# A hybrid decoder step on one core: gated products in halves, a sum split from its matmul, and one tile turned a step later

## The chip, the cores and the metric

The kernel runs on one core of a Trainium2 chip. The metric is device time in microseconds (us) of one execution. The core's engines are named as in the profile: PE is TensorE's matmuls and PEld its weight loads, DVE is VectorE, ACT is ScalarE, POOL is GpSimd, and SP is SyncE, whose queue issues nearly all transfers.

## The reference

The kernel computes one layer of a decoder trunk for 1024 prompt rows and 8 sample rows (one new row for each of 8 sequences), all in float32, with a model width of 1024. Cut to what matters:

```python
xn = _rmsnorm(h, pre_g)
proj = jnp.einsum('bld,de->ble', xn, w_in)          # w_in is 1024 x 7168
u, v, z_a, x_b, z_b, g_a, g_b = jnp.split(proj, SPLITS, axis=-1)
u = jax.nn.gelu(u)
vn = _layernorm(jax.nn.gelu(v), ln_g, ln_b)
y_a = u * _chunk_spatial_mix(vn, w_s, b_s) * jax.nn.silu(z_a)
pooled, new_pool = _pool_branch(x_b, prev_pool, pos0, w_pool, pool_scale)
y_b = pooled * jax.nn.silu(z_b)
m = sigmoid(g_a) * (y_a @ w_pa) + sigmoid(g_b) * (y_b @ w_pb)
h = h + _rmsnorm(m @ w_out, post_g)
h = h + _rmsnorm(sigmoid(_rmsnorm(h, ple_in_g) @ w_pg) * (p @ w_ple), ple_out_g)
```

Three places of it concern the change. The first is the gated branch, `y_a`: a product of three factors for every channel and row. The second is the pool branch of the sample rows, whose trailing windows reach back into the last 15 rows of each sequence (`state_pool`); their sums over the window are needed. The third is the second norm of h and the product with `w_pg`, whose operand is h turned to have channels on the partitions.

## The kernel before

**Tiles and products.** Everything is cut into tiles of 128 partitions. Activations stand turned, channels on partitions and rows along the free axis: a block of 128 channels is 128 x 1032, for 1024 prompt rows and 8 sample rows. A pair of two such blocks of the result is computed by Strassen's seven products, whose operands are sums and differences of quarters of the weights and of the activations (names such as T1 to T4, B11, B21, B22 are such quarters or sums: `xT3` is one of the activations, `wgB21` one of `w_pg`). The operands are split in a high and a low part (`h` and `l` in a name), and three matmuls are done for each pair. In a timeline a product is a run of 12 matmuls 512 wide, or of 24 that are 260 wide where the half with the sample rows is concerned. Each product lands in a region of PSUM of two banks, of which three rotate (`acc`, in the last two products `acct`), and is added into its result by DVE or ACT: an instruction such as `u<-acc,u` does that, and the region may be written again afterwards. Two more single banks serve everything else (`pht`, `state`, `mix`).

**What DVE does for the products.** It makes the operands' sums and low parts (`zaw`, `zas`, `uw`, `us`, `hw`, `hs`, 512 wide each), the sums into results, and the elementwise work.

**The gated branch.** Class ZA (from line 1060) is what becomes of the results z_a. `done` (lines 1063 to 1073) multiplies, for each of the two 128-channel blocks of a pair, z by u (128 x 1032), makes the mixed block, multiplies z's 1024 prompt columns with it, and its 8 sample columns with the samples' mix. There are four pairs, so eight blocks. In the timeline these are the rows `za<-za,u` and `za<-za,big`.

**The past rows.** `pool_state` (line 1087) sets a 128 x 1024 space to zero and loads the past rows of the 8 sequences into it by small transfers. `state_sums` (line 1103) adds them up along the free axis (a TENSOR_REDUCE from 128 x 1024 to 128 x 128), and multiplies the result on PE with the constant `twice`, which adds two halves of the partitions and turns the result; then DVE copies it to `past`.

**h, turned.** After the product with `w_out` the tiles of h are finished two at a time: `out_finish` (norm and residual), `gate_norm` (the sum of squares of the next norm), and `gate_input` (line 1441), which turns a tile: for the tiles concerned here eight 128 x 128 transposes on PE into two `pht` banks and two ACT copies to `big`. The last two tiles, 7 and 6, are turned at the first pair's products with `w_pg`.

**What sets the order.** Nothing is issued when it is written. The code calls the operations on a recorder, Planner (lines 56 to 300), which keeps what each reads and writes. `at(step, f)` attaches work f to a step, a step being one of the products in PE's sequence; the planner derives from that a due time for each operation. `order` then goes through time with a table of estimated durations and gives each engine the next operation by these due times; PE's products are fixed in their main sequence, and the rest, the transfers of SP's queue with it, fits in where the estimate says. `play` (line 296) issues it all, so nearly every row of the profile has L299. A small edit may thus reorder a wide stretch on several engines.

Of the kernel before, what the change touches and what calls it, by code (L numbers as in the profile page):

```python
# [13 lines left out]
ALU = mybir.AluOpType  # L14

P = 128
D = 1024
NB = D // P
# [282 lines left out]
@with_exitstack  # L301
def tile_hybrid_step(ctx, tc, *args):
    hybrid_step(ctx, tc, *args)


def hybrid_step(
# [7 lines left out]
    nc = tc.nc  # L314
# [24 lines left out]
    def bank(name):  # L339
        n_name[0] += 1  # L340
        return plan.tile(bankp.tile([P, 512], F32, tag="bank", name=f"{name}_{n_name[0]}"), "bank")
# [22 lines left out]
    def mul(out, a, b):  # L364
        nc.vector.tensor_tensor(out=out, in0=a, in1=b, op=ALU.mult)
# [6 lines left out]
    nc = plan  # L372
# [6 lines left out]
    big = cpool.tile([P, NB, T], F32, tag="big", name="big")  # L379
# [34 lines left out]
    class Operand:  # L414
# [37 lines left out]
        def at(self, what, k):  # L452
            return [part[:, k % 2, :] for part in self.parts[what, k // 2]]
# [144 lines left out]
    def halves(t, j):  # L598

        return Features.like(t[:, HALF:]) if j else t[:, :HALF]  # L600
# [90 lines left out]
    class User:  # L691
# [37 lines left out]
        def done(self):  # L729
            pass  # L730
# [63 lines left out]
    def sample_stationary(src, nk, gain=None):  # L794

        st = slot("sst", (P, nk, P), F32R)
        nc.gpsimd.memset(f32(st), 0.0)
        ps = bank("psst").rearrange("p (k t) -> p k t", t=16)
        for k in range(nk):
            nc.tensor.transpose(ps[:, k, :NS], src[:NS, k * P : (k + 1) * P], ident[:NS, :NS])  # L800
        got = ps[:, :nk, :NS]
        if gain is not None:
            mul(smix_s, got, gain.unsqueeze(2).to_broadcast([P, NB, NS]))
            got = smix_s
        split(got, st[:, :, :NS], st[:, :, 32 : 32 + NS])
        return st
# [54 lines left out]
    NPAIR = NB // 2  # L861
# [198 lines left out]
    class ZA(User):  # L1060
        func = AF.Silu

        def done(self):
            u = us.pop(self.pair)
            for m, z in enumerate(self.out):
                b = 2 * self.pair + m
                mul(z, z, u[m])
                zt, mixed = z[:, :SEQ].rearrange("p (t c) -> p t c", c=P), big[:, :, b * P : (b + 1) * P]
                nc.vector.scalar_tensor_tensor(out=mixed, in0=mixed, scalar=lncol[:, 0, b : b + 1],
                                               in1=lnt["off"][:, b].unsqueeze(1).to_broadcast([P, NB, P]),  # L1070
                                               op0=ALU.mult, op1=ALU.add)
                mul(zt, zt, mixed)
                mul(z[:, SEQ:], z[:, SEQ:], smix_s[:, b, :])

        def store(self):
# [24 lines left out]
    state_sb, tail = big[:, 7, :D], big[:, 6, :D]  # L1100
    past = cpool.tile([P, NB, NS], F32, tag="past", name="past")

    def state_sums():

        got = big[:, 4, :P]
        nc.vector.tensor_reduce(out=got, in_=state_sb.rearrange("p (r c) -> p c r", c=P),
                                op=ALU.add, axis=mybir.AxisListType.X)
        ps = bank("state")
        nc.tensor.matmul(ps[:, : P // 2], got, twice, start=True, stop=True)
        nc.vector.tensor_copy(past, ps[:, : P // 2].rearrange("p (b t) -> p b t", b=NB))  # L1110
# [121 lines left out]
    bsteps, xusers = [], []  # L1232
# [5 lines left out]
    flat, c = big.rearrange("p b t -> p (b t)"), [T + 4 * w for w in (0, HALF, HALF + WIDE, HALF + 2 * WIDE)]  # L1238
# [20 lines left out]
    c = vsteps[0]  # L1259
# [11 lines left out]
    for i, u in enumerate(vusers):  # L1271

        nxt = vsteps[1][1:] + vsteps[2] if i == 0 else (vsteps[i + 1] if i + 1 < NPAIR else gasteps[0])
# [20 lines left out]
    for i, z in enumerate(zausers):  # L1294
        at(uflow[14 * (i + 1) + 1], z.store)
    at(bsteps[0][0][2], pool_state)
    at(bsteps[0][0][4], state_sums)
    for g, u in enumerate(xusers):
        at(bsteps[g][1][4], u.tails)
        for i in range(2):  # L1300
# [26 lines left out]
    p, l, c = gbsteps[2], gbsteps[3], pasteps[0]  # L1327
    turn_over(yaop, l, [*l[1:], c[0]])
    p, l, c = pasteps[2], pasteps[3], pbsteps[0]
# [78 lines left out]
    def out_finish(t):  # L1408
        r = rows(t)
        h = h_of[t][:r]  # L1410
        rs = rstd(parts.pop(t), r)
        nc.vector.scalar_tensor_tensor(out=h, in0=h, scalar=rs[:r], in1=gains["post"][:r],
                                       op0=ALU.mult, op1=ALU.mult)
        nc.gpsimd.dma_start(out=h, in_=x_of(t), accum_op=ALU.add)
        dma(kept["h"][t * P : t * P + r, :], h)
# [5 lines left out]
    def words_of(t):  # L1421
        return big.bitcast(U16)[:, :, 2 * t * P : 2 * (t + 1) * P]

    def gate_norm(t):

        r = rows(t)
        h = h_of[t]
        n, spare = sm("ssq"), slot("hspare", (P, D))[:r] if t == S else big[:, :, t * P : (t + 1) * P]
        src = h[:r] if t == S else h.rearrange("p (k c) -> p k c", c=P)
        nc.scalar.activation(out=spare, in_=src, func=AF.Square, scale=D ** -0.5, accum_out=n[:r])  # L1430
        root(n, r, rin(t))
        if t not in BY_DMA:
            return
        words = slot("hw", (P, 2, D), U16)
        for w in range(2):
            nc.scalar.activation(out=words[:, w], in_=h.bitcast(U16).rearrange("p (c w) -> p w c", w=2)[:, w],
                                 func=AF.Copy)
        h_of[t] = h.bitcast(U16).rearrange("p (k t) -> p k t", t=P)
        nc.sync.dma_start_transpose(out=h_of[t], in_=words.rearrange("p w c -> p (w c)"))

    def gate_input(t):

        got = h_of.pop(t)
        if t == S:
            samples["h"] = sample_stationary(got, NB)
            return
        for k4 in (slice(0, 4), slice(4, NB)):
            if t in BY_DMA:
                nc.scalar.activation(out=words_of(t)[:, k4].rearrange("p k (t w) -> p k t w", w=2),
                                     in_=got.rearrange("p (w k) t -> p k t w", w=2)[:, k4], func=AF.Copy)  # L1450
                continue
            ps = bank("pht")
            for k in range(4):
                nc.tensor.transpose(ps[:, k * P : (k + 1) * P], got[:, (k4.start + k) * P : (k4.start + k + 1) * P], ident)
            nc.scalar.activation(out=big[:, k4, t * P : (t + 1) * P], in_=ps.rearrange("p (k t) -> p k t", t=P),
                                 func=AF.Copy)
# [72 lines left out]
    def embed_gate_sample():  # L1529
        ge_start(S)  # L1530
        for j, o in enumerate(sample_product(samples["h"], wgop)):
# [9 lines left out]
    gatesteps = [strassen(Turned(i, "h"), wgop, Embed(i), Tokens, LAST if i == NPAIR - 1 else None)  # L1541
                 for i in range(NPAIR)]
# [5 lines left out]
    l, c = pbsteps[3], outsteps[0]  # L1548
    turn_over(woop, l, [*l[2:], c[0], c[1]], ("B11", "T3", "T2", "B21", "T4", "T1", "B22"))
    l, c = outsteps[3], gatesteps[0]  # L1550
# [13 lines left out]
    for i in range(NPAIR):  # L1564
        nxt = outsteps[i + 1] if i + 1 < NPAIR else gatesteps[0]
        ts = [2 * i + 1, 2 * i]
        at(nxt[0], lambda ts=ts: [out_finish(t) for t in ts])
        at(nxt[1], lambda ts=ts: [gate_norm(t) for t in ts])
        at(nxt[6], lambda ts=ts: [gate_input(t) for t in ts])


    we = Moving(w_ple, 2, "we")
# [200 lines left out]
```

## Time and profile before

| | |
|---|---|
| median of 3 runs | 991.16 us (990.98 to 991.76) |
| the profiled execution's own time | 991.0 us |
| its span, first to last instruction | 989.3 us |
| granted TensorE clock, mean | 0.998 |
| busy: PE, PEld, DVE, ACT, POOL | 975.0, 875.3, 797.4, 529.6, 69.9 us |
| transfers | 174.53 MB, mean 176 GB/s |

The profile is of one execution. A timeline row gives start, duration, engine, line, operation, what is written and read (buffer numbers left out), the shapes, and how many equal instructions the row holds; in brackets stands idle time of the engine before it and what ended it. Matmuls overlap in the array, so a row's duration is longer than the distance to the next one's start; the starts tell the rate. A view of waits lists, for an engine, which waits were ended by what: total us, how often, the longest.

### The profile page before, as it was taken

The numbers are of one execution on the slowest core, as the hardware profiler recorded it, in microseconds if no ns is written. First come the engines' busy times: TensorE is split into PE (matmuls) and PEld (weight loads), VectorE is DVE, ScalarE is ACT, GpSimd is POOL, SyncE is SP. The second block draws the span as 40 slices with busy tenths as digits, with TensorE's granted clock in tenths as the row PEclk, the third lists the DMA queues.
The fourth block names the chain that finished last, engine by engine and source line by source line (L and its number), as shares of the span: only waits on it lengthen the run. The fifth ranks groups of instructions, "written<-read, shape, count | busy, mean of one in ns | idle before, by whom it ended". The sixth has DMA issues, their size and how long they took to land. (4 is left out here: it accounts for less than half of the span.)

```text
span 989.3 us, 15945 instructions
## 1 busy us (share of the span) xinstructions
PE 975.0 (99%) x6087; PEld 875.3 (88%) x6087; DVE 797.4 (81%) x1239; ACT 529.6 (54%) x888; POOL 69.9 (7%) x142
## 2 busy tenths in 40 slices
PE   8999999999999999999999999999999999999996
PEld 7789999999998999999999999999999988888885
DVE  6796568787769888979897987697799899779696
ACT  7778987565434433344442333562353365877463
POOL 2100001000000000000000100000000001313111
PEclk9999999999999999999999999999999999999999
DMA  9335553322374354556735075973663552699546
GB/s 339 132 104 117 120 151 128 129 85 75 120 256 149 125 202 142 215 197 213 255 124 191 17 268 207 315 281 131 228 244 124 177 191 63 133 299 361 149 109 191
DMA packets 109291, 174.53 MB, mean 176 GB/s; under 512 B 28632, under 2 KB 68016, under 8 KB 109207
## 3 DMA queue, kind: packets, MB, share of 16 engines
q1 hardware_dynamic: 107118, 166.13, 49.1%
q0 software_dynamic: 2048, 7.37, 4.4%
q8 instruction: 48, 0.79, 0.3%
q14 instruction: 29, 0.23, 0.1%
q10 hardware_dynamic: 48, 0.01, 0.0%
HBM read 114.84 MB, written 53.87 MB: 171 GB/s over the span
## 5 line engine op out<-in xcount | busy, mean ns | idle before, releaser
L299 DVE TENSOR_TENSOR u<-acc,u 128x520 f32<-128x520 f32 (+1 forms) x90 | 62.6, 696 | 37.3 <-PE acc L299 33.5
L299 POOL TENSOR_TENSOR rstd<-ms,mhalf 128x1 f32<-128x1 f32 (+1 forms) x36 | 32.3, 900 | 193.5 <-DVE ms L299 183.8
L299 POOL MEMSET u<- 128x8 f32 x35 | 4.0, 150 | 499.9 <-PE acc L299 235.8
L299 ACT ACTIVATE u<-acc 128x512 f32<-128x512 f32 x39 | 23.2, 595 | 25.6 <-PE acc L299 25.0
L299 ACT ACTIVATE paw<-pas 128x512 fp32r<-128x512 f32 x16 | 10.1, 629 | 30.0 <-DVE pas L299 24.8
L299 ACT ACTIVATE pbw<-pbs 128x512 fp32r<-128x512 f32 x16 | 10.0, 628 | 28.0 <-DVE pbs L299 24.8
L299 DVE TENSOR_TENSOR big<-big 128x1024 f32<-128x1024 f32 (+4 forms) x20 | 23.6, 1218 | 0.0
L299 ACT ACTIVATE big<-mix 128x256 f32<-128x256 f32 x32 | 12.1, 383 | 19.1 <-PE mix L299 16.8
L299 PE MATMUL accm<-qh,wpoolw 128*128 128x260 f32 (+1 forms) x96 | 20.9, 319 | 0.0
L299 ACT ACT_TABLE_LOAD x13 | 16.7, 1283 | 7.2 <-PE acc L299 6.2
L299 ACT ACTIVATE big<-v 128x1024 uint16<-128x1024 uint16 x16 | 18.5, 1175 | 3.8 <-DMA v<-vw 3.8
L299 ACT ACTIVATE zbw<-zbs 128x512 fp32r<-128x512 f32 x16 | 10.1, 628 | 16.7 <-DVE zbs L299 11.8
L299 DVE TENSOR_TENSOR v<-acc,u 128x520 f32<-128x520 f32 (+1 forms) x9 | 6.3, 697 | 15.4 <-PE acc L299 15.4
L299 DVE TENSOR_TENSOR acc<-acc,u 128x512 f32<-128x512 f32 (+1 forms) x16 | 11.2, 699 | 8.7 <-PE acc L299 8.7
L299 ACT ACTIVATE gbw<-gbs 128x512 fp32r<-128x512 f32 x16 | 10.0, 626 | 15.0 <-DVE gbs L299 12.8
L299 ACT ACTIVATE zaw<-zas 128x512 fp32r<-128x512 f32 x16 | 10.0, 630 | 14.6 <-DVE zas L299 9.1
L299 ACT ACTIVATE uw<-us 128x512 fp32r<-128x512 f32 x16 | 10.0, 626 | 13.7 <-DVE us L299 11.1
L299 PEld LDWEIGHTS accm<-qh,wpoolw 128*128 128x128 f32 x96 | 15.6, 188 | 1.9
L299 DVE TENSOR_TENSOR big<-mix,big 128x256 f32<-128x256 f32 x32 | 12.7, 420 | 5.5 <-ACT big L299 5.1
L299 ACT ACTIVATE gb<-gb 128x1032 f32<-128x1032 f32 (+1 forms) x8 | 6.8, 854 | 19.0 <-DVE gb L299 19.0
L299 ACT ACTIVATE vw<-v 128x1024 uint16<-128x1024 uint16 x16 | 16.1, 1046 | 0.5 <-DVE v L299 0.5
L299 ACT ACTIVATE big<-h 128x1024 f32<-128x1024 f32 (+1 forms) x12 | 13.0, 1092 | 5.0 <-DMA h<-in_x_prompt_dram 5.0
(690 smaller groups left out, 3623.5 us busy)
## 6 DMA issues: line engine op xcount, KB each, us to landing
ga<-ga SPq DMA_DIRECT2D x16, 516.0 KB
gb<-gb SPq DMA_DIRECT2D x16, 516.0 KB
ya<-za SPq DMA_DIRECT2D x8, 516.0 KB
yb<-zb SPq DMA_DIRECT2D x8, 516.0 KB
x<-in_x_prompt_dram SPq DMA_DIRECT2D x8, 512.0 KB
vraw<-in_w_in_dram SPq DMA_DIRECT2D x8, 512.0 KB
e<-e SPq DMA_DIRECT2D x8, 512.0 KB
garaw<-in_w_in_dram SPq DMA_DIRECT2D x8, 512.0 KB
```

The source lines that it names most:

```text
L299: getattr(getattr(self.nc, e), method)(*args, **kwargs)
```

## The change

There are three parts. In `ZA.done` the two long multiplications of each block are each done as two of half the length (512 and 520 columns for the first, 512 and 512 for the second): two instructions more for each of the eight blocks' multiplications, 16 in all. `state_sums` is cut in two: the reduction (`state_reduce`) stays at the fifth step of the first pool product, and the matmul and the copy go two steps later. And of the last pair of tiles of h, the second, tile 6, is turned not at the same step as tile 7 (the last of the first group of `w_pg` products) but at the first step of the next group.

```diff
             for m, z in enumerate(self.out):
                 b = 2 * self.pair + m
-                mul(z, z, u[m])
+                for j in range(2):
+                    mul(halves(z, j), halves(z, j), halves(u[m], j))
...
-                mul(zt, zt, mixed)
+                for ts in (slice(0, NB // 2), slice(NB // 2, NB)):
+                    mul(zt[:, ts], zt[:, ts], mixed[:, ts])
                 mul(z[:, SEQ:], z[:, SEQ:], smix_s[:, b, :])
...
-    def state_sums():
-
-        got = big[:, 4, :P]
+    got = big[:, 4, :P]
+
+    def state_reduce():
+
         nc.vector.tensor_reduce(out=got, in_=state_sb.rearrange("p (r c) -> p c r", c=P),
                                 op=ALU.add, axis=mybir.AxisListType.X)
+
+    def state_sums():
+
         ps = bank("state")
         nc.tensor.matmul(ps[:, : P // 2], got, twice, start=True, stop=True)
...
-    at(bsteps[0][0][4], state_sums)
+    at(bsteps[0][0][4], state_reduce)
+    at(bsteps[0][0][6], state_sums)
...
-        at(nxt[6], lambda ts=ts: [gate_input(t) for t in ts])
+        at(nxt[6], lambda ts=ts: gate_input(ts[0]))
+        at(nxt[6] if i + 1 < NPAIR else gatesteps[1][0], lambda ts=ts: gate_input(ts[1]))
```

The planner turns this into a new order. Four pieces of it follow; a name's number tells one buffer from the next of the same name, and `x2` that a row stands for two instructions.

DVE around the add of product acc_614 into u_605, in the third pair of the gated branch (za_590 and za_591 are the pair's two blocks, zas and zaw operands of later products). Before:

```order
368 L299 TENSOR_TENSOR u_605<-acc_609,u_605 128x520
369 L299 TENSOR_TENSOR us_600<-uraw_585 128x512
370 L299 TENSOR_TENSOR us_600<-uraw_586,us_599 128x512
371 L299 TENSOR_TENSOR uw_603<-us_600,uw_603 128x512
372 L299 TENSOR_TENSOR zaw_615<-zaraw_606,zaw_615 128x512
373 L299 TENSOR_TENSOR zas_618<-zaraw_606,zaraw_607 128x512
374 L299 TENSOR_TENSOR zas_618<-zas_618,zaraw_606 128x512
375 L299 TENSOR_TENSOR za_590<-za_590,u_569 128x1032
376 L299 TENSOR_TENSOR uw_613<-us_600,uw_613 128x512
377 L299 TENSOR_TENSOR zaw_617<-zas_618,zaw_617 128x512
378 L299 TENSOR_TENSOR za_590<-za_590,big 128x1024
379 L299 TENSOR_TENSOR u_605<-acc_614,u_605 128x520
```

Now:

```order
375 L299 TENSOR_TENSOR za_590<-za_590,u_569 128x520
376 L299 TENSOR_TENSOR u_605<-acc_609,u_605 128x520
377 L299 TENSOR_TENSOR za_590<-za_590,big 128x512 x2
378 L299 TENSOR_TENSOR za_590<-za_590,smixs 128x8
379 L299 TENSOR_TENSOR za_591<-za_591,u_570 128x512
380 L299 TENSOR_TENSOR zaw_615<-zaraw_606,zaw_615 128x512
381 L299 TENSOR_TENSOR zas_618<-zaraw_606,zaraw_607 128x512
382 L299 TENSOR_TENSOR zas_618<-zas_618,zaraw_606 128x512
383 L299 TENSOR_TENSOR za_591<-za_591,u_570 128x520
384 L299 TENSOR_TENSOR zaw_621<-zaraw_607,zaw_621 128x512
385 L299 TENSOR_TENSOR u_605<-acc_614,u_605 128x520
```

The long products on za_590 no longer stand right ahead of the add; they are halves now, and most stand earlier. On PE the product acc_614 has changed places with acc_616 and comes first.

DVE some thirty microseconds earlier, around the column sums of w_out (woraw_541 and 542, 559 and 560, 575 and 576 are pairs of loaded blocks; zaw_581 is the low part of an operand of a product acc_583). Now:

```order
340 L299 TENSOR_TENSOR woraw_560<-woraw_560,woraw_559 128x512
341 L299 TENSOR_TENSOR woraw_576<-woraw_576,woraw_575 128x512
342 L299 TENSOR_TENSOR u_569<-acc_580,u_563 128x520
343 L299 TENSOR_TENSOR woraw_575<-woraw_575 128x512
344 L299 TENSOR_TENSOR zaw_581<-zaraw_565,zaw_581 128x512
345 L299 TENSOR_TENSOR woraw_575<-woraw_576,woraw_575 128x512
346 L299 TENSOR_TENSOR zaw_587<-zaraw_565,zaw_587 128x512
```

Before, zaw_581 stood at row 328 and zaw_587 at 336, ahead of all rows of woraw_559, 560, 575 and 576, which began at row 340.

DVE around the reduction of the past rows (state). Before:

```order
474 L299 TENSOR_TENSOR zbw_703<-zbs_700,zbw_703 128x512
475 L299 TENSOR_TENSOR zbs_700<-zbraw_685,zbs_699 128x512
476 L299 TENSOR_TENSOR xb_692<-acc_696,u_683 128x512
477 L299 TENSOR_REDUCE big<-big 128x128
478 L299 TENSOR_TENSOR xb_692<-acc_701,u_683 128x520
```

Now:

```order
485 L299 TENSOR_TENSOR za_671<-za_671,smixs 128x8
486 L299 TENSOR_TENSOR zbs_699<-zbraw_685,zbs_698 128x512
487 L299 TENSOR_REDUCE big<-big 128x128
488 L299 TENSOR_TENSOR xb_692<-acc_696,u_683 128x512
489 L299 TENSOR_TENSOR zbw_703<-zbs_699,zbw_703 128x512
490 L299 TENSOR_TENSOR xb_692<-acc_700,u_683 128x520
```

The reduction has gone ahead of the add of acc_696 and of the operand zbw_703. PE's matmul on its result stands where it stood.

PE where the last two tiles of h are turned (h_1397 is tile 7, h_1379 tile 6). Before:

```order
3350 L299 MATMUL acct_1460<-wgB22h_1434,hw_1452 128x512
3351 L299 MATMUL pht_1468<-ident,h_1397 128x128 x4
3352 L299 MATMUL pht_1469<-ident,h_1397 128x128 x4
3353 L299 MATMUL pht_1470<-ident,h_1379 128x128 x4
3354 L299 MATMUL pht_1471<-ident,h_1379 128x128 x4
3355 L299 MATMUL acct_1480<-wgT2h_1389,hw_1457 128x512
```

Now:

```order
3350 L299 MATMUL acct_1460<-wgB22h_1434,hw_1452 128x512
3351 L299 MATMUL pht_1468<-ident,h_1397 128x128 x4
3352 L299 MATMUL pht_1469<-ident,h_1397 128x128 x4
3353 L299 MATMUL acct_1480<-wgT2h_1389,hw_1457 128x512
3354 L299 MATMUL acct_1480<-wgT2l_1390,hw_1457 128x512
```
```order
3362 L299 MATMUL acct_1480<-wgT2h_1391,hw_1457 128x512
3363 L299 MATMUL pht_1473<-ident,h_1379 128x128 x4
3364 L299 MATMUL pht_1474<-ident,h_1379 128x128 x4
3365 L299 MATMUL acct_1471<-wgB21h_1399,hw_1464 128x512
```

The whole product acct_1480 now stands between the two tiles' transposes.

## The prediction

> **What bounds the kernel now.** I read the page first, then the busy time by stretch, then TensorE's waits, and last the timeline around the waits that the change can reach. The page's first lines:
>
> ```profile
> span 989.3 us, 15945 instructions
> PE 975.0 (99%) x6087; PEld 875.3 (88%) x6087; DVE 797.4 (81%) x1239; ACT 529.6 (54%) x888; POOL 69.9 (7%) x142
> ```
>
> TensorE (PE) is busy 99% of the span, and a busy PE is all but the whole time. The stretches, start-up, middle and tail, say how much it idles where (columns: length, then busy time of PE, PEld, DVE, ACT, POOL, clock, DMA share, GB/s):
>
> ```profile
> 0.00:41.00 41.00, 37.00 (x201) 30.77 (x201) 25.69 (x47) 29.08 (x48) 8.92 (x35) 1.00 0.74 269
> 41.00:980.50 939.50, 937.68 (x5885) 844.37 (x5886) 767.18 (x1184) 498.47 (x836) 60.41 (x106) 1.00 0.53 172
> 980.50:989.30 8.80, 0.32 (x3) 0.12 (x2) 4.57 (x10) 2.07 (x6) 0.59 (x1) 0.78 0.46 179
> ```
>
> The change touches neither the first row (4.0 us idle) nor the last (the chain behind the last matmul). In the middle PE idles 939.50 − 937.68 = 1.82 us in all. The clock is 1.00 there, so no edit can win by a higher one. TensorE's waits by what ended them:
>
> ```profile
> PE warm L299 <- POOL ident masks.py:199: 1.9, 1, 1.9
> PE e L299 <- ACT big L299: 1.4, 1, 1.4
> PE pst L299 <- DVE ms L299: 0.9, 1, 0.9
> PE acc L299 <- DVE u L299: 0.5, 1, 0.5
> PE pht L299 <- ACT big L299: 0.3, 1, 0.3
> PE state L299 <- DVE big L299: 0.2, 1, 0.2
> PE acc L299 <- DVE ga L299: 0.2, 1, 0.2
> ```
>
> The first three are start-up. Of the rest, three answer to the three parts of the diff: acc on u (a product whose PSUM region the add into u must empty), state on big (the column sums of the past rows), and pht on big (the second tile of h being transposed). They are 0.5 + 0.2 + 0.3 us of idle. A stall costs somewhat more than its idle time, because back-to-back matmuls overlap: I measure it from start to start below.
>
> **Part 1, the multiplications in halves.** VectorE (DVE) around the wait, then PE:
>
> ```profile
> 311.16 0.69 DVE L299 TENSOR_TENSOR u<-acc,u 128x520 f32<-128x520 f32 x1
> ...
> 316.13 1.23 DVE L299 TENSOR_TENSOR za<-za,u 128x1032 f32<-128x1032 f32 x1
> 317.28 0.69 DVE L299 TENSOR_TENSOR uw<-us,uw 128x512 fp32r<-128x512 f32 x1
> 317.88 0.69 DVE L299 TENSOR_TENSOR zaw<-zas,zaw 128x512 fp32r<-128x512 f32 x1
> 318.48 1.22 DVE L299 TENSOR_TENSOR za<-za,big 128x1024 f32<-128x1024 f32 x1
> 319.62 1.42 DVE L299 TENSOR_TENSOR u<-acc,u 128x520 f32<-128x520 f32 x2
> ```
> ```profile
> 316.60 0.40 PE L299 MATMUL acc<-xT3h,uw 128*128 128x260 f32 x2
> ...
> 319.23 0.40 PE L299 MATMUL acc<-xT1l,uw 128*128 128x260 f32 x2
> 319.46 0.40 PE L299 MATMUL acc<-xT1h,uw 128*128 128x260 f32 x2
> 320.36 0.50 PE L299 MATMUL acc<-xB11h,zaw 128*128 128x512 f32 x1 [0.51 <-DVE u L299]
> 320.70 0.40 PE L299 MATMUL acc<-xB11l,zaw 128*128 128x512 f32 x1
> ```
>
> Two 260-wide matmuls take 319.46 − 319.23 = 0.23 us from start to start, so xB11 was due at 319.70 and began at 320.36: 0.66 us. It waited for the first of the two adds at 319.62 (u_605<-acc_614), which lasts 0.69, and that add stood in DVE's order behind the two long za products. The matmul after the stall is slow too: 320.70 − 320.36 = 0.34, where the same form elsewhere takes 288.89 − 288.66 = 0.23:
>
> ```profile
> 288.66 0.39 PE L299 MATMUL acc<-xB21h,zaw 128*128 128x512 f32 x1
> 288.89 0.40 PE L299 MATMUL acc<-xB21l,zaw 128*128 128x512 f32 x1
> ```
>
> That restart is 0.11 us, which may go as well: **0.66 to 0.77 us**.
>
> In the changed order the products on za_590 stand before u_605<-acc_614, but in halves and much earlier, and PE runs the product acc_614 one place sooner, ahead of acc_616. acc_614 is the xT3 product, complete at 316.60 + 0.40 = 317.0 before; acc_616, which now runs behind it, is twelve 512-wide matmuls, 12 × 0.23 = 2.8 us, so acc_614 is complete near 314.2. In DVE's order eight rows of 0.60 (317.88 − 317.28) and an 8-wide one now stand between u_605<-acc_609, which was added at 311.16, and u_605<-acc_614: below 5 us. If the first add stays where it was, the second starts by 311.16 + 0.60 + 5.0 = 316.8 and ends by 317.5, against 319.70 wanted: 2.2 us of room, and more if acc_609 is added sooner, where the room was −0.7.
>
> What the halves cost: a 1032-wide product takes 317.28 − 316.13 = 1.15 us from start to start and a 512-wide one 0.60, so a split costs 2 × 0.60 − 1.15 = 0.05 us. Sixteen come to 0.8 us of DVE. DVE has 939.50 − 767.18 = 172 us free in the middle stretch, and some of it just there:
>
> ```profile
> 288.95 0.70 DVE L299 TENSOR_TENSOR u<-acc,u 128x520 f32<-128x520 f32 x1 [1.95 <-PE acc L299]
> 294.47 0.70 DVE L299 TENSOR_TENSOR u<-acc,u 128x520 f32<-128x520 f32 x1 [4.82 <-PE acc L299]
> ```
>
> DVE waited for PE there, not PE for DVE, so I cost the splits at nothing; with that cover gone they would be the 0.8 us. The Trainium skill's page "Perfetto Trace Analysis", section "Optimizing Scalar/DVE Operations", has a rule on either side: about 60 ns of overhead for each DVE instruction on SBUF speaks for larger operations where the engine is saturated, and breaking instructions up is advised where it is not and yet causes bubbles elsewhere. By its figure the sixteen splits would be 16 × 0.06 = 1.0 us (an estimate) against the 0.8 from the rows; the 4.82 us idle row puts this stretch under the second half of the rule.
>
> The halves also let the planner move other work. The column sums of w_out (woraw) go ahead, and their loads on SP's queue with them, and this is where a new wait could arise (rival 1).
>
> **Part 2, the past rows' sum two steps ahead of its product.**
>
> ```profile
> 396.94 0.69 DVE L299 TENSOR_TENSOR zbs<-zbraw,zbs 128x512 f32<-128x512 f32 x1
> 397.54 0.69 DVE L299 TENSOR_TENSOR xb<-acc,u 128x512 f32<-128x512 f32 x1
> 398.14 1.96 DVE L299 TENSOR_REDUCE big<-big 128x128 f32<-128x1024 f32 x1
> ```
> ```profile
> 399.53 0.40 PE L299 MATMUL acc<-xT1h,xbw 128*128 128x260 f32 x2
> 400.16 0.43 PE L299 MATMUL state<-twice,big 128*128 128x64 f32 x2 [0.22 <-DVE big L299]
> ```
>
> The state matmul was due at 399.53 + 0.24 = 399.77 and began at 400.16, after the reduction's end at 400.10: **0.39 us**. PE's order around it is as it was. On DVE the reduction now stands ahead of xb<-acc,u (0.60) and so starts at 397.54 or sooner, ends by 399.5, and has 0.3 us of room. One zbw product has also gone behind it, so I expect more like 1 us. Its input, the past rows, needs to have landed by 397.5; it waits for a memset and small loads that the order issues well before, and I count them at nothing. If the reduction were only half as much sooner as I say, 0.1 us of the wait would stay. The adds behind it, which free PSUM, slip by one instruction: the xb row is now at about 399.5, its region is wanted only two products later, past 405.
>
> **Part 3, the last tile of h one step later.** ACT, then PE:
>
> ```profile
> 914.35 1.05 ACT L299 ACTIVATE big<-h 128x1024 f32<-128x1024 f32 x1
> 915.99 1.09 ACT L299 ACTIVATE big<-pht 128x512 f32<-128x512 f32 x2 [0.51 <-PE pht L299]
> ```
> ```profile
> 915.06 0.40 PE L299 MATMUL acct<-wgB22h,hw 128*128 128x512 f32 x1
> 915.30 1.04 PE L299 MATMUL pht<-ident,h 128*128 128x128 f32 x8
> 916.64 1.04 PE L299 MATMUL pht<-ident,h 128*128 128x128 f32 x7 [0.31 <-ACT big L299]
> ```
>
> The second eight transposes need a PSUM bank that ACT had to empty, and ACT could not begin before 915.99. Running matmuls overlap by 0.40 − 0.24 = 0.16 to 0.17 us (915.06 and 915.30), so without the wait they would have begun at 915.30 + 1.04 − 0.17 = 916.17; they began at 916.64: **0.47 us**. Now the product acct_1480<-wgT2, twelve matmuls and 2.8 us, runs between the two tiles. The second tile's transposes come at 916.17 + 2.77 = 918.9; the two evacuations that free the banks ended at 915.99 + 1.09 = 917.08. Room 1.9 us. What moves is eight transposes on PE and two evacuations on ACT; no DMA is in gate_input for this tile. What is late next is the sums on the turned tile, needed a product or more later than the transposes; I see over 0.5 us of room there, and in wgT2's own operand hw, which PE now asks for at 916.2 in place of 917.5.
>
> **Sum.** 0.66 + 0.39 + 0.47 = 1.52, with the restart 1.63, and with a similar restart behind the state matmul at most 1.75. I take 1.6. The profiled execution took 991.0 us, 989.3 of them span and 1.7 around it; it becomes 989.4 with a span of 987.7. The median of the three runs is 991.16, 0.16 above, so I say **989.5 us**, −0.17%. A difference below 0.2% (2.0 us) can't be told from none in a measurement of this kernel, and it lies below that. The middle stretch also caps it: 1.82 us of idle, of which these three are 1.04 and the rest is made up of pieces that the diff does not reach.
>
> **Rivals.** *1, a new wait on the loads of w_out.* SP issues nearly all DMAs in order. These rows show how a load fares in a burst there:
>
> ```profile
> 273.11 0.33 SPq L299 DMA_DIRECT2D wohigh<-woraw  x1
> ...
> 287.20 2.30 SPq L299 DMA_DIRECT2D uraw<-in_w_in_dram  x2
> 295.64 0.64 ACT L299 ACTIVATE uw<-uraw 128x512 fp32r<-128x512 f32 x1 [3.44 <-DMA uraw<-in_w_in_dram]
> ```
>
> A load issued at 287.20 was used at 295.64, 8.4 us on. In the changed order DVE's row woraw_576<-woraw_576,woraw_575 stands ahead of u_569<-acc_580, woraw_575 and zaw_581, and the matmuls from 289.1 on read zaw_581. Four rows of 0.60 and 0.1 of latency before that, so the pair must land by 286.6. The loads follow the write of the first pair (wohigh, at 273.11 before). DVE now finishes that pair after some 13.3 us of rows behind the last add into za_545 instead of 10.1, so near 276.5, and the loads are issued by 277.5; with the 8.4 us of the row at worst they land at 285.9, room 0.7 us, and with 6 us, which I hold likelier, at 283.5. It decides against the change when they land later than 286.6 + 1.6 + 2.0 = 290.2, since each us beyond 286.6 stops PE for one: near 13 us for a load, not seen in these rows. At 291 it would be 989.5 + 4.4, about 994 us. For it speaks that DVE's order is strict; against it that the queue is less full at 277 than at 287. A milder form, a landing 1 to 3 us late, is a wash: 990.5 to 992.5.
>
> *2, the stalls only move.* The wide reordering brings other late adds on DVE or ACT, of the same 0.3 to 0.7 us size, and the 0.8 us of splits is not hidden. One or two of them leave 990.2 to 991.2. For it: 1.82 us of idle is already nearly nothing, and any new order has pieces of 0.2; against it: the rooms I found are mostly over 1 us.
>
> *3, more goes than I count.* If the wait on ga (0.2 idle) or other overlaps lost around these places go too, a further 0.35 us is enough for 989.1 and "faster"; the order near the ga wait is untouched, which speaks against it.
>
> **How the numbers follow.** The forecast (all three stalls gone, no new one) 0.56, giving 989.2 to 990.0; rival 2 with the mild form of rival 1 together 0.22 (990.2 to 992.5); rival 3 0.15 (988.8 to 989.1); rival 1 in full 0.07 (994). The runs before spread over 0.8 us, so a part of the forecast, 0.06, falls below the bound at 989.18, and of the second group a part, 0.03, lies above 993.1 or close to it. Faster 0.15 + 0.06 = 0.21; slower 0.07 + 0.03 = 0.10; same 0.69. The range 988.8 to 991.3 leaves out the tail of the second group and rival 1.
>
> **What would show it.** Right: no wait of PE's acc on u near 320, none of state on big near 400, none of pht on big near 917; PE's middle idle at about 0.8 us; DVE with 16 instructions more and about 0.8 us more busy; a span of 987.6 to 987.8. Wrong in part 1: PE waiting near 289 to 295 for a zaw that stands behind a woraw row with idle time put down to a DMA. Wrong in part 2: the reduction starting later than 397.9. Wrong in part 3: a wait on an hw or on big between 916 and 925. A span unchanged with all three waits gone would mean that start-to-start excess is not time on the path, and my reading of PE as the bound would fall.

## The result, and the profile after

Over 22 runs each, the changed kernel takes 989.57 us by the median (988.87 to 990.72) and the kernel before 991.66 (990.98 to 993.07). The ratio is 0.9978, with a 95% interval of 0.9972 to 0.9985. That is 2.1 us by the medians: small, but clear of the noise, since the interval lies below 1 and the slowest run of the changed kernel is below the fastest of the kernel before.

The page of the changed kernel, its middle stretch, and all of TensorE's waits but three small ones of the start-up:

```profile
span 988.0 us, 15969 instructions
PE 974.5 (99%) x6087; PEld 874.7 (89%) x6087; DVE 797.4 (81%) x1255; ACT 530.2 (54%) x888; POOL 70.4 (7%) x142
```
```profile
41.00:979.20 938.20, 937.04 (x5885) 843.85 (x5886) 767.56 (x1201) 499.38 (x837) 60.58 (x106) 1.00 0.54 173
```
```profile
PE warm L299 <- POOL ident masks.py:199: 1.9, 1, 1.9
PE e L299 <- ACT big L299: 1.4, 1, 1.4
PE pst L299 <- DVE ms L299: 0.9, 1, 0.9
...
PE acc L299 <- DVE ga L299: 0.2, 1, 0.2
...
```

The waits of acc on u, state on big and pht on big are gone, and no new one has come. From PE's first matmul after the ga wait (146.12 before, 146.51 after) to its last (980.54 before; 979.26 after) it is 834.42 us before and 832.75 after, 1.67 less, and PE's idle time in that stretch falls from 1.08 to 0.01 us. Ahead of that point the changed kernel's profiled execution is 0.39 later, in start-up work that the change does not touch. The row above hides this: its stretch begins at a fixed 41 us, and the start-up wait of e on big, which ends at 41.95 in place of 41.55, puts 0.40 us more of idle into it, so that its idle time falls only from 1.82 to 1.16. The three places, first DVE and PE near 320:

```profile
313.20 0.69 DVE L299 TENSOR_TENSOR zas<-zaraw,zaraw 128x512 f32<-128x512 f32 x1 [0.29 <-DMA zaraw<-in_w_in_dram]
...
315.75 0.69 DVE L299 TENSOR_TENSOR u<-acc,u 128x520 f32<-128x520 f32 x1
```
```profile
319.97 0.40 PE L299 MATMUL acc<-xT1h,uw 128*128 128x260 f32 x2
320.22 0.39 PE L299 MATMUL acc<-xB11h,zaw 128*128 128x512 f32 x1
320.44 0.40 PE L299 MATMUL acc<-xB11l,zaw 128*128 128x512 f32 x1
```

The add ends at 316.44, 3.8 us ahead, and the restart of 0.34 has gone too. The reduction (DVE), and the state matmul:

```profile
396.37 2.00 DVE L299 TENSOR_REDUCE big<-big 128x128 f32<-128x1024 f32 x1
```
```profile
399.55 0.33 PE L299 MATMUL state<-twice,big 128*128 128x64 f32 x2
399.69 0.48 PE L299 MATMUL acc<-xB11h,zbw 128*128 128x512 f32 x1
```

It ends at 398.37, 1.2 us ahead. Tile 7's copies on ACT, and tile 6's transposes:

```profile
915.32 1.06 ACT L299 ACTIVATE big<-pht 128x512 f32<-128x512 f32 x2
```
```profile
918.22 1.04 PE L299 MATMUL pht<-ident,h 128*128 128x128 f32 x8
```

The copies end at 916.38, 1.8 us ahead.

### The profile page after: what moved, and what is told of

It is laid out like the page before. It is cut to its first block, busy times and chain, and to the rows that moved or that the text cites. A ratio compares the mean times of both kernels' runs of the same rounds, so it can differ in the third digit from the quotient of the medians.

```text
span 988.0 us, 15969 instructions
## 1 busy us (share of the span) xinstructions
PE 974.5 (99%) x6087; PEld 874.7 (89%) x6087; DVE 797.4 (81%) x1255; ACT 530.2 (54%) x888; POOL 70.4 (7%) x142
## 5 line engine op out<-in xcount | busy, mean ns | idle before, releaser
L299 ACT ACTIVATE u<-u 128x1032 f32<-128x1032 f32 (+1 forms) x8 | 6.8, 852 | 18.6 <-DVE u L299 18.5
```

Source lines behind the costliest of these rows:

```text
L299: getattr(getattr(self.nc, e), method)(*args, **kwargs)
```

## The experiments

All times are medians beside runs of the kernel before on the same chip; the ratio is an estimate of its own, with its 95% interval, and can differ from the quotient of the medians by up to 0.07%. "Wait A" is the one near 320, B that of state near 400, C that of pht near 916; sizes are from start to start, as in the prediction.

**Each part alone.** The edits are the three parts of the diff, one at a time, each on the kernel before.

> Part 1 alone: the two long products of the gated branch in halves; the state sum and tile 6 as before. Theory of the stalls (the time falls by the start-to-start excess of the stalls that are gone, and by nothing else): the wait near 320 goes (0.66 to 0.77 us). The planner's new order also puts the reduction of the past rows ahead of the add of acc_696, so the state wait (0.39) should go or shrink too, although part 2 is not there; the pht wait of 0.31 us idle near 915 stays. Time -0.7 to -1.2 us against the kernel before, ratio near 0.999. Rival, each part removes its own stall: the state wait of 0.2 us idle is still there, -0.7. Rival, the reshuffle: the whole gain of the full change (2.1 us by the medians) comes from part 1.

> Part 2 alone: the reduction and its matmul two steps apart. In the order that the planner makes of it, the reduction does not go ahead on DVE (it still follows the add of acc_696, and one more operand), but the matmul on PE goes back by two products, 5.7 us. Theory of the stalls: the state wait is gone by the later matmul, not by an earlier sum: -0.39 us, the waits near 320 and 916 as before. Rival, no gain: a wait of the same size appears at the matmul's new place or at the copy into past: 0.0.

> Part 3 alone: tile 6 of h turned one step later. Theory of the stalls: the pht wait is gone, -0.47 us, the waits near 320 and 400 as before, and none new on an operand hw. Rival, the wait moves to the turned tile's sums: 0.0.

Measured: part 1 alone 989.82 us beside 991.51, ratio 0.9980 (0.9971 to 0.9989); part 2 alone 991.22, 0.9994 (0.9985 to 1.0003); part 3 alone 990.94, 0.9992 (0.9983 to 1.0001). The reduction and the state matmul with part 1 alone:

```profile
396.43 2.00 DVE L299 TENSOR_REDUCE big<-big 128x128 f32<-128x1024 f32 x1
```
```profile
399.28 0.33 PE L299 MATMUL state<-twice,big 128*128 128x64 f32 x2
```

Part 1 alone removes A and B, as the theory of the stalls had it; only C is left. The rival that each part removes its own stall has fallen, and so has, with C still there, the one that part 1 makes the whole gain. The times of parts 2 and 3 alone can't be told from no change, as both intervals reach 1; what these parts do is read from the traces. Part 1 alone gained 1.7 us, more than the 1.2 expected. Why shows in the other two runs, whose order near 320 is that of before. TensorE's wait A in part 2 alone, then in part 3 alone:

```profile
PE acc L299 <- DVE u L299: 1.2, 1, 1.2
```
```profile
PE acc L299 <- DVE u L299: 0.8, 1, 0.8
```

It was 0.5 us of idle in the profile of before. Up to that wait the rows of DVE, ACT and SP stand in the same order in all three profiles. The same instructions in the same order thus have a wait A of 0.66, 1.00 and 1.33 us in three executions; **it is not a constant, and the profile that I had read held the smallest**. A larger A also costs its size: PE's stretch from the ga wait to its end is 1.92 us longer than the changed kernel's in part 2 alone, where A, C and the restart of 0.11 come to 1.91, and 1.35 longer in part 3 alone, where A, B and the restart come to 1.50. B is gone with part 2 alone and C with part 3 alone, as expected. With part 2 alone the reduction is no earlier; the state matmul is some 6 us later:

```profile
399.52 2.00 DVE L299 TENSOR_REDUCE big<-big 128x128 f32<-128x1024 f32 x1
```
```profile
406.63 0.33 PE L299 MATMUL state<-twice,big 128*128 128x64 f32 x2
```

**Parts 1 and 3 without part 2.** The edit leaves out the second part of the diff.

> Parts 1 and 3 of the change without part 2. Theory: the new order that the halves bring already puts the reduction ahead of its matmul, so nothing is lost: no state wait near 400, the time as the changed kernel's, 989.4 to 989.9. Rival, part 2 has its own share: the wait of 0.2 us idle is back, +0.39 us.

Measured: 989.36 us beside 991.81, ratio 0.9976 (0.9967 to 0.9985), no state wait (one of 0.2 us on xb near 493 stands in this profile instead, as smaller ones do in two others). Beside part 1, part 2 adds nothing that can be seen.

**The order, by hand.** Part 3, and this on DVE instead of parts 1 and 2:

```diff
-TENSOR_TENSOR za_590<-za_590,big 128x1024
 TENSOR_TENSOR u_605<-acc_614,u_605 128x520
+TENSOR_TENSOR za_590<-za_590,big 128x1024
...
-TENSOR_TENSOR xb_692<-acc_696,u_683 128x512
 TENSOR_REDUCE big<-big 128x128
+TENSOR_TENSOR xb_692<-acc_696,u_683 128x512
```

> Part 3, and the order of before with two instructions of DVE moved by hand in place of parts 1 and 2: the undivided product on za_590 goes behind the add of acc_614, the add of acc_696 behind the reduction. No instruction is split, no transfer moves before 900 us. Theory of the stalls: all three waits are gone, and the time falls as in the full change, -1.5 to -1.7 us, PE idle in the middle 1.1 to 1.2 us. Rival, the halves or the wide reordering themselves gain: this kernel gains 0.5 us (part 3) and no more. The reduction ends at 399.5 by the timeline of before, 0.2 us ahead of its matmul, so some 0.1 to 0.2 us of the state wait may stay.

Measured: 990.26 beside 991.51, ratio 0.9987 (0.9978 to 0.9996): 1.25 us, less than the theory and more than the rival. B and C are gone, A is down to 0.18 us, but a successor has come, three microseconds later on PE:

```profile
323.85 0.48 PE L325 MATMUL acc<-xB22h,uw 128*128 128x260 f32 x2 [0.60 <-ACT zaw L325]
```

The next product's operand zaw is late in turn (0.76 us from start to start). So halves are not needed to remove B and most of A, but one swap does not settle the place.

**Halves in the old order.** Each long product is issued as two, where the one stood:

```diff
-TENSOR_TENSOR za_590<-za_590,u_569 128x1032
+TENSOR_TENSOR za_590<-za_590,u_569 128x512
+TENSOR_TENSOR za_590<-za_590,u_569 128x520
```

> The order of before on every engine, but each of the 16 long products of the gated branch is issued as two halves in its old place. What the order does is so taken away from what the halves do. Theory, the gain is in the order: three such products stand ahead of the add of acc_614 in the stretch where VectorE is busy without a gap, so the add comes 3 x 0.05 = 0.15 to 0.2 us later and the wait near 320 grows by that; the other waits stay; time +0.1 to +0.3 us against the kernel before. Rival, halves gain by themselves: -0.7 us or better.

Measured: 992.12 beside 991.73, ratio 0.9999 (0.9990 to 1.0008), wait A 1.20 us, B and C as before. In their old places they cost a little: from the zas row to the add it is 4.96 us (315.49 to 320.45), where the kernel before has 4.82. Halves alone gain nothing; the gain is in the order that the planner makes of them.

**What sets wait A.** ACT and DVE of part 3 alone (the order of before) show where the add's lateness begins:

```profile
313.45 0.63 ACT L299 ACTIVATE zaw<-zaraw 128x512 fp32r<-128x512 f32 x1 [0.59 <-DMA zaraw<-in_w_in_dram]
```
```profile
314.12 0.69 DVE L299 TENSOR_TENSOR zaw<-zaraw,zaw 128x512 fp32r<-128x512 f32 x1 [0.53 <-ACT zaw L299]
314.82 0.69 DVE L299 TENSOR_TENSOR zas<-zaraw,zaraw 128x512 f32<-128x512 f32 x1
...
319.64 1.42 DVE L299 TENSOR_TENSOR u<-acc,u 128x520 f32<-128x520 f32 x2
```

ACT waits for the load of zaraw, DVE for ACT, and the add follows 4.82 us behind the zas row, in each of the three profiles with this order. In the changed kernel that distance is 315.75 − 313.20 = 2.55, without the two long products. Four runs took this apart. The first two move the loads on SP's queue:

```diff
+DMA zaraw_606<-in_w_in_dram          load_early
 DMA wolow<-woraw_592
 DMA wohigh<-woraw_593
-DMA zaraw_606<-in_w_in_dram
 DMA zaraw_607<-in_w_in_dram
...
+DMA zaraw_606<-in_w_in_dram          writes_behind
+DMA zaraw_607<-in_w_in_dram
 DMA wolow<-woraw_592
 DMA wohigh<-woraw_593
-DMA zaraw_606<-in_w_in_dram
-DMA zaraw_607<-in_w_in_dram
```

> The order of before with one transfer moved: the load of zaraw_606 goes ahead of the two writes of w_out's last parts on SP's queue, and is so issued near 305.8 (when its space comes free) in place of 308.1. The profiles of before, tile6_alone and state_alone show ACT waiting 0.24, 0.59 and 1.11 us for this load and the wait near 320 growing with it (0.66, 1.00, 1.33). Theory, a saturated stretch: VectorE is busy 15.5 of the 16 us from 304 to 320, so the load only adds what VectorE idles for it; without it about 0.4 to 0.5 us of the wait stay. Time -0.2 to -0.6 us. Rival, the load is the cause: the wait is gone altogether, -0.7 to -1.3 us.

Measured: 991.97 beside 991.73, ratio 1.0000 (0.9991 to 1.0009), and A was 1.29 us. Both theories missed: the first load came earlier, but DVE then waited for the second, which still went out behind the writes:

```profile
315.61 0.69 DVE L322 TENSOR_TENSOR zas<-zaraw,zaraw 128x512 f32<-128x512 f32 x1 [0.91 <-DMA zaraw<-in_w_in_dram]
```

> The order of before with the two writes of w_out's last part (wolow, wohigh of woraw_592 and 593) moved on SP's queue from ahead of the two loads of zaraw to right behind them; VectorE's order as it was. The earlier runs put the add of acc_614 4.8 us behind VectorE's first zas row, and that row behind the landing of both zaraw loads, which go out behind four writes in a row. Theory, landing plus chain: the second load goes out near 307.7, not behind 2 of the 4 writes, zas starts as soon as VectorE gets there (314.3 to 314.6), the wait near 320 comes down to 0.3 to 0.6 us and is the same in each execution; time -0.2 to -0.7 us. Rival, the load alone: the wait is gone, -0.8 to -1.3. Rival, not the load: 0.8 us or more, 0.0.

Measured: 991.13 beside 991.81, ratio 0.9994 (0.9985 to 1.0003); A is 0.28 us, and DVE no longer waits for a load. The interval reaches 1, so the trace has to show this too; C happens to be 0.3 us larger in this profile (0.6 us of idle), for a reason that was not looked for.

```profile
306.19 2.43 SPq L323 DMA_DIRECT2D zaraw<-in_w_in_dram  x2
```
```profile
314.24 0.69 DVE L323 TENSOR_TENSOR zaw<-zaraw,zaw 128x512 fp32r<-128x512 f32 x1
314.85 0.69 DVE L323 TENSOR_TENSOR zas<-zaraw,zaraw 128x512 f32<-128x512 f32 x1
...
319.66 1.42 DVE L323 TENSOR_TENSOR u<-acc,u 128x520 f32<-128x520 f32 x2
```

The 0.28 is what DVE's own chain leaves here; what stands above it in the other profiles is thus put down to the landing. The other two runs take DVE's work away from the stretch:

```diff
-TENSOR_TENSOR woraw_593<-woraw_593,woraw_592 128x512
-TENSOR_TENSOR woraw_592<-woraw_592 128x512
-TENSOR_TENSOR woraw_592<-woraw_593,woraw_592 128x512
-TENSOR_TENSOR woraw_593<-woraw_593,woraw_592 128x512
...
 TENSOR_TENSOR uw_636<-us_637,uw_636 128x512
+(the same four)                       sums_later; left out in sums_left_out
```

In the first the two writes on SP go with them, behind the loads.

> The order of before with the four column sums of the last part of w_out (woraw_592, woraw_593) moved on VectorE from 306 to about 335, and the two writes that follow them moved on SP's queue behind the loads of zaraw; nothing else, no halves. Theory, a saturated stretch: 2.6 us of VectorE's work leave the stretch ahead of 320, the add of acc_614 follows the end of its product at 317.0, and the wait near 320 is gone without a new one on zaw near 323; the waits near 400 and 916 stay. Time -0.7 to -1.4 us. Rival, the halves or the exchange of the products acc_614 and acc_616 on TensorE are needed: 0.3 us or more of the wait stay, as with one product moved by hand.

Measured: 994.62 beside 991.73, ratio 1.0022 (1.0012 to 1.0031), slower. A is gone, but two new waits have come, each longer than A is in the three profiles: 1.64 us on zaw at 323 and 1.48 on za at 345, from start to start. DVE's row of zas at 323.38 now idles 3.19 us for PE, perhaps for space, as the moved parts hold theirs some 30 us longer; that this is the reason is not shown.

> The kernel before without the four column sums of the last part of w_out on VectorE, 2.6 us of work between 304 and 308; the parts are written as they were loaded, so this part of w_out's products is computed from other numbers. No space is held longer, unlike the run in which these sums were moved. Theory, landing plus chain: VectorE reaches zas 2.6 us sooner or at the landing, near 313; the add ends by 318.9, the wait near 320 is gone, and no successor on an operand zaw near 323 comes, since that chain is early too. Time -0.7 to -1.4 us. Rival, the wait moves on to 323 whenever it is taken away without the halves: less than 0.3 us gained.

Measured: 991.79 beside 991.81, ratio 0.9998 (0.9989 to 1.0007), and A is 1.40 us. My theory failed here. DVE got there early and waited:

```profile
310.87 0.69 DVE L321 TENSOR_TENSOR uw<-us,uw 128x512 fp32r<-128x512 f32 x1
315.01 0.69 DVE L321 TENSOR_TENSOR zaw<-zaraw,zaw 128x512 fp32r<-128x512 f32 x1 [3.45 <-ACT zaw L321]
```
```profile
305.10 0.33 SPq L321 DMA_DIRECT2D wohigh<-woraw  x1
305.52 0.38 SPq L321 DMA_DIRECT2D wolow<-woraw  x1
306.00 0.74 SPq L321 DMA_DIRECT2D wohigh<-woraw  x1
306.83 2.47 SPq L321 DMA_DIRECT2D zaraw<-in_w_in_dram  x2
```

ACT's row of zaw began at 314.35. The profile names PE for its wait, but with the sums moved the same row began at 311.24, when PE was no further on, so it was the load that came last. Without the sums the four writes of 0.5 MB went out closer together, right ahead of the loads, and the loads landed no sooner. DVE with 2.6 us less to do gains nothing while the loads stand behind the writes; with the loads ahead of two of the writes, 0.28 us of A is left with DVE's work as it was. **So A is a landing, behind writes, followed by a chain on DVE.** The change acted on both: two of the four writes went out 14 us earlier, the loads 2 us earlier, and the long products left the chain. SP, before and then after:

```profile
302.90 0.33 SPq L299 DMA_DIRECT2D wolow<-woraw  x1
304.94 0.33 SPq L299 DMA_DIRECT2D wohigh<-woraw  x1
307.00 0.32 SPq L299 DMA_DIRECT2D wolow<-woraw  x1
307.72 0.32 SPq L299 DMA_DIRECT2D wohigh<-woraw  x1
308.13 1.87 SPq L299 DMA_DIRECT2D zaraw<-in_w_in_dram  x2
```
```profile
290.74 0.32 SPq L299 DMA_DIRECT2D wohigh<-woraw  x1
...
303.82 0.33 SPq L299 DMA_DIRECT2D wolow<-woraw  x1
305.63 0.33 SPq L299 DMA_DIRECT2D wohigh<-woraw  x1
306.06 1.32 SPq L299 DMA_DIRECT2D zaraw<-in_w_in_dram  x2
```

Each of the two was tried by itself in the old order, and either does most of it: the loads ahead of two writes leave 0.28 us of A, and one long product taken out of the chain leaves 0.18, although ACT still waited 0.95 us for the load there (the order by hand, with its new wait at 323). A third difference, that acc_614 comes one product sooner on PE, was not tried apart.

**The price of a split.** Each half as two quarters, in the changed kernel's order.

> The changed kernel's order with each half of the long products issued as two quarters in the same place, 32 VectorE instructions more. It prices the splits that the prediction costed at nothing. Theory, hidden: VectorE is busy 1.6 to 2 us more in all, none of TensorE's waits comes back (the rooms were 4 us near 320 and 1.2 near 400), time as the changed kernel's, 989.4 to 989.9. Rival, VectorE is the bound by now: +1 to +2 us.

Measured: 989.47 us beside 991.81, ratio 0.9977 (0.9968 to 0.9986), no wait back. DVE is busy 1.8 us more for 32 instructions, 0.056 us each (roughly, since profiles with the same work on DVE differ by up to 0.5 us in it):

```profile
PE 974.0 (99%) x6087; PEld 874.7 (89%) x6087; DVE 799.2 (81%) x1287; ACT 530.6 (54%) x888; POOL 70.5 (7%) x142
```

**The first rival, brought about.** In the changed kernel the load of woraw_576 goes from behind that of woraw_575 to behind that of uraw_586 on SP.

> The changed kernel with one transfer moved: the load of woraw_576 goes four places later on SP's queue, behind the load of uraw_586, so that it is issued near 283.9 in place of 278.5 and lands near 291.5 in place of 285.0. This is the first rival of the prediction, brought about on purpose. Theory: VectorE's rows woraw_576, u_569, woraw_575 and zaw_581 follow the landing, zaw_581 ends near 294.3 in place of 288.3, and the matmuls that want it at 289.5 wait: 4.5 to 5 us more than the changed kernel, 994 us or 2.5 to 3.0 us more than before. Rival, the room is larger than I think: less than 1 us more than the changed kernel.

Measured: 997.27 us beside 991.73, ratio 1.0049 (1.0035 to 1.0063): 7.7 us more than the changed kernel's 989.57, where 4.5 to 5 had been expected. The wait came where and as large as expected (5.0 us from start to start):

```profile
289.06 0.39 PE L322 MATMUL acc<-xB21l,zaw 128*128 128x512 f32 x1
294.30 1.22 PE L322 MATMUL acc<-xB21h,zaw 128*128 128x512 f32 x2 [4.85 <-DVE zaw L322]
```

About 2.4 of the other 2.7 us are a clock: twelve matmuls came 0.43 us apart in place of 0.23 (the stretches ahead of, in and behind the wait, PEclk third from the right):

```profile
280.00:289.00 9.00, 9.00 (x65) 8.47 (x65) 2.78 (x5) 2.09 (x3) 0.00 (x0) 1.00 1.03 358
289.00:294.30 5.30, 0.45 (x3) 0.02 (x2) 2.56 (x5) 1.22 (x3) 0.00 (x0) 0.87 0.24 95
294.30:299.50 5.20, 5.20 (x12) 4.13 (x13) 5.05 (x9) 1.64 (x4) 0.00 (x0) 0.50 0.60 217
299.50:305.00 5.50, 5.50 (x37) 4.97 (x35) 3.00 (x5) 3.93 (x6) 0.00 (x0) 0.98 0.48 180
```

## Why the prediction was right, and where it was not

- **What bounds the kernel.** Right. PE from 146 us to its end lost 1.67 us, against the 1.63 of the three stalls with the restart, and the time came to 989.57, against 989.5. DVE's busy time grew by 1.8 us (quarters) and shrank by about 3 (sums left out) without moving the time. Three of the signs named for it missed. The span is 988.0, not 987.6 to 987.8, and the middle's idle time 1.16, not 0.8, both by the 0.4 us of start-up; DVE's busy time is 797.4 as before, not 0.8 more.
- **Part 1, size.** The term of 0.66 to 0.77 us was right for the execution that I read and too small for the kernel: the step "it was due at 319.70 and began at 320.36" took one landing for a constant. In two more profiles with that order A is 1.00 and 1.33. By the medians of 22 runs the gain is 2.1 us, 0.5 more than my sum; with the mean A of the three profiles, 1.00, the sum would be 1.97. That A made the difference is inferred from this, as only one of the 22 runs has a profile. The predicted time stood all the same because the median of three runs that I started from, 991.16, was itself 0.5 below the median of 22, 991.66: two errors that cancelled, which is luck.
- **Part 1, cause.** "That add stood in DVE's order behind the two long za products" named the later half of the chain. I had not followed it back to the landing of zaraw and the writes ahead of it on SP, although DVE's and ACT's rows just ahead show it.
- **Splits at nothing.** Right for the changed kernel: 0.05 us each was the estimate, 0.056 measured, and even three times as many cost no time. The reason given was wrong in place: the idle rows of DVE shown for it lie at 287 to 294 us, while in the 16 us ahead of 320 DVE was busy for 15.5. There the splits do cost time when they stay in the old order (0.14 us more ahead of the add); the new order is what makes room for them. The Trainium skill's page "Perfetto Trace Analysis", section "Optimizing Scalar/DVE Operations", gives about 60 ns for an instruction; the trace agrees. The page's advice that breaking up instructions may let work finish sooner where an engine is not saturated holds here only through the order: the same halves in the old order gave a ratio of 0.9999.
- **Part 2.** The 0.39 us is gone, but the step that puts it down to part 2 was wrong. Part 1's order does it alone, and part 2 alone does it by a later matmul, not an earlier sum. A similar restart behind the state matmul, my upper end, wasn't one: that matmul's successor still takes 0.32 us with no wait ahead of it (399.69 to 400.01).
- **Part 3.** Right in room (1.8 us, 1.9 forecast), and part 3 alone removes C and nothing else. The size fits: PE's stretch is 0.38 us longer with part 1 alone, where C is the only one of the three left, than in the changed kernel, against the 0.47 read.
- **Rival 1.** It did not happen. The load was in by the start of the first row below, 1.2 us ahead of the 286.6 that I had as the limit, zaw_581 ended at 288.30, and the matmul that reads it began at 289.52 without a wait. The two loads went out from 277.9 on, so the last was in 7.5 us later at most, not the 6 held likelier, and DVE idled 2.32 us ahead of its row. DVE in the changed kernel:

```profile
285.39 0.69 DVE L299 TENSOR_TENSOR woraw<-woraw,woraw 128x512 f32<-128x512 f32 x1 [2.32 <-issue]
286.39 0.70 DVE L299 TENSOR_TENSOR u<-acc,u 128x520 f32<-128x520 f32 x1 [0.31 <-PE acc L299]
287.01 0.68 DVE L299 TENSOR_TENSOR woraw<-woraw 128x512 f32<-128x512 f32 x1
287.61 0.69 DVE L299 TENSOR_TENSOR zaw<-zaraw,zaw 128x512 fp32r<-128x512 f32 x1
```

  Its mechanism was right and its price too low: a wait of 5.0 us cost 7.7, mostly since the clock fell with it.
- **Rivals 2 and 3.** Stalls did move in the orders made by hand (0.76 us at 323 in one; 1.64 and 1.48 with the sums moved), but not in the planner's. More than the sum was gained in the runs, but not as rival 3 had it: the wait on ga is still there (0.2 us), and the rest is put down to A, as above.

## What to carry to other kernels

On a kernel whose matmul engine is busy 99% of the time, the start-to-start excess of the few waits left is what a new order can gain, and it added up to within 0.2 us here; but take each from several profiles, since a wait that ends a chain from a transfer varies between executions (0.66 to 1.33 us here). Follow a late instruction back past its engine's queue to the first row that waited for something else, and look at what stands ahead of that on the transfer queue: putting two loads ahead of two writes left 0.28 us of the wait, where 2.6 us less work on the late engine left all of it. And of a change in several parts, try each part alone: here one part's new order did the work of two.

## What was not expected of the hardware

After TensorE had idled for 4.85 us, the granted clock was 0.50 for the next 5.4 us or so, and 512-wide matmuls came 5.20 / 12 = 0.43 us apart instead of 0.23 (the row with x12 above). By the means of 0.87 over 5.3 us and 0.98 over 5.5 in the rows around it, the clock had fallen near 292.9, some 3.5 us after the last matmul ended at 289.45, and was back near 299.7. After waits of up to 1.5 us of idle no such slowing was seen (the clock was 1.00 behind the one of 1.48 us in the run with the sums moved); those cost some 0.1 us at the restart. The Trainium skill's page "TensorE: Matmul & The Clock Gate", section "What's actually happening", has the clock at half after an idle window of about 3.4 us and full again after a busy one, where the windows run freely. The trace agrees: half the clock from 3.5 us of idle on, and the 5.4 us of the return lie between one such window and two.
